# A hybrid encoder layer on one core: the chunk state update as one plain fp32 product, decay factors on ScalarE, the second logits product on 128 rows

## The chip, the cores and the metric

The kernel runs on one core of a Trainium2 chip. The metric is the device time of one execution in microseconds (us); lower is better. Several executions were timed and one was profiled. The core has five engines that run side by side: TensorE (PE: matrix products, with a row of its own for the loading of their stationary operand, PEld), VectorE (DVE), ScalarE (ACT), GpSimd (POOL) and SyncE (SP), which issues the transfers here. SBUF is the working memory, PSUM the memory into which TensorE writes.

## The reference, cut to what matters

One layer for two groups of tokens, 512 of a prompt and 32 of a sample, 1024 wide. A single input projection gives q, k, v for a banded attention and z, x, B, C, dt for a chunked state space scan (32 heads in 4 groups). Then come the output projections, a feed-forward block with a short convolution, and a gated product with a second embedding. The change lies in the scan and in the logits of the attention:

```python
def step(hc, inp):                       # scan over chunks, all heads
    xc, dtc, ac, bc, cc = inp
    acs = jnp.cumsum(ac, axis=1)
    seg = acs[:, :, None] - acs[:, None, :]
    decay = jnp.where(tri, jnp.exp(jnp.where(tri, seg, 0.0)), 0.0)
    cb = jnp.einsum('bign,bjgn->bijg', cc, bc)
    dx = dtc[..., None] * xc
    y = jnp.einsum('bijg,bijgr,bjgrp->bigrp', cb, decay, dx)
    y = y + jnp.einsum('bign,bgrpn->bigrp', cc, hc) * jnp.exp(acs)[..., None]
    last = acs[:, -1]
    wj = jnp.exp(last[:, None] - acs)[..., None] * dx
    h_new = hc * jnp.exp(last)[..., None, None] + jnp.einsum('bjgn,bjgrp->bgrpn', bc, wj)
    return h_new, y

def attend(q, k, v, bias):
    logits = jnp.einsum('bihd,bjhd->bhij', q, k) * (HEAD_DIM_A ** -0.5)
    probs = jax.nn.softmax(logits + bias[None], axis=-1)
    return jnp.einsum('bhij,bjhd->bihd', probs, v)
```

## The kernel before

Features lie on the partitions and the 544 tokens along the free dimension, in two halves of 272. A dense product is a list of steps; one step makes 128 output features, and is cut into pieces of 128 input features. Both operands are split into a high and a low part of a reduced fp32 type (`F32R`), and a piece (`mm3`) is six products of 128 rows and 272 columns: high by high, low by high, high by low, each for two halves. The weights are split as they arrive: ScalarE casts the high part (`wh`, L250), VectorE or GpSimd subtracts it (`wl`, L254), one unit of eight pieces ahead of its use.

All products are issued in one written order on TensorE (class `Ordered` chains them). The order of the other engines is made by a scheduler from the order of the program. The dense steps are the filling: `dense.run(n)` puts n pieces between two parts of other work. So the program has three stretches. In the scan stretch 20 passes (4 groups by 5 chunks, the fifth being the sample) are laid between dense pieces: `ssd_a` of a pass, 7 pieces, `ssd_b` of the pass before, 6 pieces. In the attention stretch parts of the attention (`att_a`: logits and softmax, `att_b`: transposes of the probabilities, `att_c`: their product with v) are laid between dense pieces in the same way. The rest is dense products alone.

`ssd_a` of one pass: C·B and a transpose of B go to one PSUM tile (`cbt`, one of four of a ring that all such work shares, `sps`); L625 masks the first into `cbm`. Four transposes give x by tokens (`xst`), from which L636 makes `dx` and `wj`. `wj` and the transposed B are split in a high and a low part (L627, L628, L640, L641). For each half of the heads the cumulated decay exponents of the chunk, broadcast over the partitions, are loaded (`ab`, L647); four subtractions with a minimum (L651, VectorE, one per head), an exponential (L652, ScalarE) and a product with the mask (L653, VectorE) make `m`; L657 and L658 make the factor for the state from `ab`. `dx`, `wj`, `m`, `ab` and their parts are tiles of one ring of 14 (`half_tile`). `ssd_b`: the y products (`yps`) from `m`, `dx`, `ab` and the state, L684 adds them to x, three products make the new state's share (`st`, L688), and L691 and L693 update the state `h`.

`stack` prepares a head's logits: on the 128 rows of `ks` the high part of k stands twice, and on those of `qs` the high and the low part of q, so that one product of 128 rows gives two of the three. The third, high part of q by low part of k, is a product over the 64 rows of the head itself (L849); the low parts of both heads of a pair share one tile `kl`, each on its own 64 rows.

Of the kernel before, what the change touches and what calls it, by code (L numbers as in the profile page):

```python
# [9 lines left out]
F32 = mybir.dt.float32  # L10
F32R = mybir.dt.float32r
AF = mybir.ActivationFunctionType
# [104 lines left out]
def trunk(ctx: ExitStack, tc: tile.TileContext, a):  # L117
# [433 lines left out]
    def bias_vector():  # L551
        er = const.tile([16, EROW], F32, name="er")
        nc.sync.dma_start(er[:, 383:EROW], a["rb"])
        V.tensor_scalar(er[:, 383:EROW], er[:, 383:EROW], -1.0, None, op0=MUL)
        V.tensor_copy(er[:, 0:383], er[:, 383:384].to_broadcast([16, 383]))
        nc.sync.dma_start(evec, er)
        for h in range(16):
            dense.defer(16 + 16 * h, lambda h=h: bias_rows(h))
# [52 lines left out]
    def ssd_a(g, c):  # L611
# [11 lines left out]
        PE.transpose(sm[:Q, 128:256], b[:, tk], ident)  # L623
        cbm = spt([128, 128], "cbm", 2)
        V.tensor_tensor(cbm[:Q, :Q], sm[:Q, 0:Q], tri[:Q, :Q], op=MUL)  # L625
        bth, btl = (pools["sp"].tile([128, 128], F32R, tag=n, name=n, bufs=2) for n in ("bth", "btl"))
        S.copy(bth[:Q], sm[:Q, 128:256])  # L627
        V.tensor_tensor(btl[:Q], sm[:Q, 128:256], bth[:Q].bitcast(F32), op=SUB)  # L628
        xp = sps("xst")
# [8 lines left out]
        dxf = dx.rearrange("p a b -> p (a b)")  # L638
        wjh, wjl = half_tile("wjh", F32R), half_tile("wjl", F32R)
        S.copy(wjh[:Q], wj[:Q])  # L640
        G.tensor_tensor(wjl[:Q], wj[:Q], wjh[:Q].bitcast(F32), op=SUB)  # L641
        sts = [(l[:Q], r.rearrange("p a b -> p (a b)")[:Q]) for l, r in ((bth, wjh), (bth, wjl), (btl, wjh))]
        ms, cps = [], []
        for hh in range(2):
            ab = half_tile("ab")
            src = asc[c, 8 * g + 4 * hh : 8 * g + 4 * hh + 4, 0:Q]
            nc.sync.dma_start(ab[:, :, :Q], src.unsqueeze(0).to_broadcast([128, 4, Q]))  # L647
            m = half_tile("m")
            for i in range(4):
                hd = 8 * g + 4 * hh + i  # L650
                V.tensor_scalar(m[:Q, i, :Q], ab[:Q, i, :Q], tm[:Q, 1, c, hd : hd + 1], 0.0, op0=SUB, op1=MIN)  # L651
            S.activation(m[:Q, :, :Q], m[:Q, :, :Q], AF.Exp)  # L652
            V.tensor_tensor(m[:Q, :, :Q], m[:Q, :, :Q],  # L653
                            cbm[:Q, :Q].unsqueeze(1).to_broadcast([Q, 4, Q]), op=MUL)
            ms.append(m)
            if inter:
                S.activation(ab[:, :, :Q], ab[:, :, :Q], AF.Exp)  # L657
                G.tensor_tensor(ab[:, :, :Q], ab[:, :, :Q],  # L658
                                cc[:, tk].unsqueeze(1).to_broadcast([128, 4, Q]), op=MUL)
                cps.append(ab)  # L660
        return dxf, sts, ms, cps

    def ssd_b(g, c, dxf, sts, ms, cps):
# [23 lines left out]
        for n, (l, r) in enumerate(sts):  # L687
            PE.matmul(st, lhsT=l, rhs=r, start=n == 0, stop=n == 2)  # L688
        hn = spt([128, 512], "h", 4)
# [113 lines left out]

    stk = {}

    def stack(m, hi):
# [4 lines left out]

        kl = st(512, "kl") if hi == 0 else stk[0][2]
        a0, b0 = 64 * hi, 64 - 64 * hi
# [9 lines left out]
    def att_a(m, i):  # L823
# [15 lines left out]
        for hi in range(2):  # L839
# [5 lines left out]
            else:  # L845
                qs, ks, kl = stk[hi]
                sl = slice(n - 256, n - 128)
                PE.matmul(L[:, :n], lhsT=qs[:, sl], rhs=ks[:, 0:n], start=True, stop=False)
                PE.matmul(L[:, :n], lhsT=qs[own, sl], rhs=kl[own, 0:n], start=False, stop=True)  # L849
            Ls.append(L)  # L850
# [295 lines left out]
    todo = [(m, i) for m in range(NPAIR) for i in range(-1 + m % 2, 4)]  # L1146
    prev = None
    att_load(0)
    stack(0, 0)
# [114 lines left out]
```

## Time and profile before

| | us |
|---|---|
| median of 3 runs | 1412.58 (1412.04 to 1417.83) |
| the profiled execution | 1413.28 |
| its span, from the first to the last instruction | 1411.2 |
| TensorE busy | 1376.0 (98%) |
| VectorE busy | 916.0 (65%) |
| ScalarE busy | 613.4 (43%) |
| GpSimd busy | 352.1 (25%) |

An engine's busy time is a mean over stretches with different limits, so it is read by stretch. Products on TensorE are pipelined: the distance between the starts of two that follow each other says what one costs, not its duration. A product in plain fp32 has two records in the trace.

### The profile page before, as it was taken

To read this page: it belongs to the slowest core of one execution; us is meant where nothing else is said; L and a number is where in the kernel's file an instruction comes from. 1 tells how busy PE (TensorE), PEld (TensorE's weight loads), DVE (VectorE), ACT (ScalarE), POOL (GpSimd) and SP (SyncE) were. 2 spreads that over 40 slices of the span, in tenths; PEclk is the share of its full clock that TensorE was granted. 3 is DMA by queue.
4 is the path that set the end of the run, shared out by engine and by line. 5 is a ranking of instruction groups with operands and counts; after the bars stand their busy time and mean duration, and the time that the engine had idled before them with its cause. 6 is when DMAs were issued, how large, how long until landed. Compare 5 with 4: busy or idle time off the path is not lost.

```text
span 1411.2 us, 26759 instructions
## 1 busy us (share of the span) xinstructions
PE 1376.0 (98%) x11065; PEld 1324.1 (94%) x11065; DVE 916.0 (65%) x1654; ACT 613.4 (43%) x1016; POOL 352.1 (25%) x464
## 2 busy tenths in 40 slices
PE   7998898989999999999999999999999999999998
PEld 7997897989988888889999999999999999999998
DVE  7999999996865555564355334577777537753545
ACT  5444343455566666654244223344444214432342
POOL 5466475464422112210000000023333103310000
PEclk9999999999999999999999999999999999999999
DMA  5723232323443323311222332222222232222221
GB/s 175 241 90 109 87 120 64 116 92 110 132 138 114 103 88 99 103 64 61 90 91 90 122 122 90 91 78 79 85 88 91 90 106 90 91 93 90 90 90 65
DMA packets 41929, 142.16 MB, mean 101 GB/s; under 512 B 9264, under 2 KB 13248, under 8 KB 29520
## 3 DMA queue, kind: packets, MB, share of 16 engines
q1 hardware_dynamic: 41808, 140.46, 29.6%
q8 instruction: 87, 1.43, 0.4%
q14 instruction: 34, 0.28, 0.1%
HBM read 129.27 MB, written 14.31 MB: 102 GB/s over the span
## 4 chain that ended last, share of the span: by engine, by line
PE 81%; DVE 13%; DMA 2%; ACT 2%; issue 1%; POOL 1%; SPq 0%; POOLq 0%; ACTq 0%
PE dps L130 72%; DVE m L651 3%; PE L L130 3%; DVE cv L597 2%; PE O L130 2%; DMA ab<-asc 2%; PE Tp L133 1%; DVE m L653 1%; DVE wl L254 1%; PE yps L130 1%; DVE xs L684 1%; DVE dx L636 1%; DVE wj L636 0%; PE qn L130 0%; DVE h L693 0%
## 5 line engine op out<-in xcount | busy, mean ns | idle before, releaser
L130 PE MATMUL dps<-hi,wh 128*128 128x272 f32 x2960 | 627.9, 294 | 14.9 <-DVE ext L572 14.6
L130 PE MATMUL dps<-lo,wh 128*128 128x272 f32 x2960 | 616.2, 290 | 5.3 <-DVE lo L375 5.3
L130 PE MATMUL dps<-hi,wl 128*128 128x272 f32 x2960 | 615.4, 290 | 2.3 <-DVE wl L254 1.9
L130 PEld LDWEIGHTS dps<-hi,wh 128*128 128x128 f32 x2960 | 467.4, 190 | 26.2 <-issue 18.5
L130 PEld LDWEIGHTS dps<-lo,wh 128*128 128x128 f32 x2960 | 469.0, 190 | 6.1 <-DVE lo L375 6.1
L130 PEld LDWEIGHTS dps<-hi,wl 128*128 128x128 f32 x2960 | 467.8, 189 | 3.1 <-DVE wl L254 2.5
L250 ACT CAST wh<-wr 128x1024 fp32r<-128x1024 f32 x192 | 201.2, 1048 | 379.3 <-PE dps L130 339.4
L254 DVE TENSOR_TENSOR wl<-wr,wh 128x1024 fp32r<-128x1024 f32 x173 | 213.3, 1233 | 48.2 <-ACT wh L250 43.3
L597 DVE SCALAR_TENSOR_TENSOR cv<-ext,hv,cv 128x547 f32<-128x547 f32 x72 | 76.9, 1068 | 2.7 <-ACT cv L594 2.1
L1021 DVE SCALAR_TENSOR_TENSOR ucv<-uext,vec,ucv 128x546 f32<-128x546 f32 x96 | 75.4, 785 | 4.2 <-ACT ucv L1018 2.4
L1014 POOL COPY cfo<-uext 128x2 f32<-128x2 f32 x48 | 10.4, 217 | 262.4 <-DVE uext L571 262.4
L1011 POOL MEMSET uext<- 128x2 f32 x48 | 4.6, 95 | 281.2 <-issue 281.2
L1053 DVE TENSOR_TENSOR x<-x,dps 128x544 f32<-128x544 f32 x24 | 17.3, 722 | 78.2 <-PE dps L130 78.0
L651 DVE TENSOR_SCALAR m<-ab,tm 128x128 f32<-128x128 f32 (+1 forms) x160 | 63.2, 452 | 5.3 <-DMA ab<-asc 5.3
L777 DVE CUSTOM_DVE_ANT_0 P<-L,bias 128x128 f32<-128x128 f32 (+3 forms) x64 | 30.9, 483 | 53.7 <-PE L L130 53.2
L569 DVE TENSOR_TENSOR uext<-dps,rstd 128x272 f32<-128x272 f32 x48 | 21.2, 442 | 63.1 <-PE dps L130 58.5
L254 POOL TENSOR_TENSOR wl<-wr,wh 128x1024 fp32r<-128x1024 f32 x19 | 50.8, 2672 | 44.8 <-ACT wh L250 36.8
L1015 POOL COPY cfo<-uext 128x2 f32<-128x2 f32 x48 | 55.5, 1157 | 0.0
L658 POOL TENSOR_TENSOR ab<-ab,bc 128x512 f32<-128x512 f32 (+1 forms) x32 | 42.5, 1332 | 40.1 <-ACT ab L657 37.8
L652 ACT ACTIVATE m<-m 128x512 f32<-128x512 f32 (+1 forms) x40 | 22.7, 567 | 65.8 <-DVE m L651 65.6
L733 POOL TENSOR_TENSOR ql<-qs,qh 128x544 fp32r<-128x544 f32 x16 | 22.0, 1376 | 103.6 <-ACT qh L732 91.6
L779 ACT ACTIVATE P<-P,sm 128x128 f32<-128x128 f32 (+3 forms) x64 | 36.0, 562 | 23.2 <-DVE sm L777 22.9
(246 smaller groups left out, 1626.4 us busy)
## 6 DMA issues: line engine op xcount, KB each, us to landing
wr<-in_w SPq DMA_DIRECT2D x96, 1024.0 KB, 4.9
ab<-asc SPq DMA_DIRECT2D x32, 256.0 KB, 5.5
bsc<-evec SPq DMA_DIRECT2D x16, 320.0 KB, 7.5
bias<-bsc SPq DMA_DIRECT2D x16, 256.0 KB, 3.5
xin<-in_xT SPq DMA_DIRECT2D x8, 272.0 KB, 5.4
out_o_v<-v SPq DMA_DIRECT2D x8, 272.0 KB, 2.1
out_o_k<-qk SPq DMA_DIRECT2D x8, 272.0 KB, 2.1
x<-in_xT SPq DMA_DIRECT2D x8, 272.0 KB, 4.6
```

What stands on the lines that cost most here:

```text
L130: return self._pin(nc.tensor.matmul(*args, **kw))
L250: cp = S.copy(hi, r)
L254: eng.tensor_tensor(lo, r, hi.bitcast(F32), op=SUB)
L597: V.scalar_tensor_tensor(y[:, :n], ext[:, j : j + n], hv[:, 24 * j + ti : 24 * j + ti + 1], y[:, :n], op0=MUL, op1=ADD)
L651: V.tensor_scalar(m[:Q, i, :Q], ab[:Q, i, :Q], tm[:Q, 1, c, hd : hd + 1], 0.0, op0=SUB, op1=MIN)
L652: S.activation(m[:Q, :, :Q], m[:Q, :, :Q], AF.Exp)
L658: G.tensor_tensor(ab[:, :, :Q], ab[:, :, :Q], cc[:, tk].unsqueeze(1).to_broadcast([128, 4, Q]), op=MUL)
L733: G.tensor_tensor(lo[:, :T], sq[:, :T], hi[:, :T].bitcast(F32), op=SUB)
L777: V.tensor_tensor_reduce(out=P, in0=L, in1=B, scale=1.0, scalar=3e38, op0=ADD, op1=MIN, accum_out=nm[:n])
L779: S.activation(P, P, AF.Exp, scale=-1.0, bias=nm[:n], accum_out=sm[:n])
L1015: G.tensor_copy(cfo[:, i, 2:4], ext[:, UW - 2 : UW])
L1021: V.scalar_tensor_tensor(y[:, :n], ext[:, j : j + n], vec[:, V_FW + 48 * j + i : V_FW + 48 * j + i + 1], y[:, :n], op0=MUL, op1=ADD)
```

## The change

`ssd_a`/`ssd_b`: `wj` and the transposed B are no longer split; the state product is one product of plain fp32 operands (`bt` by `wj`) instead of three of split parts. The mask is applied in place, in the PSUM tile, and L653 (L651 after the change) reads it from there. The four subtractions for `m` become four ACTIVATEs on ScalarE (Relu with scale −1 and a bias operand, L649 after the change), followed by an exponential with scale −1. `stack`: each of the two heads gets a tile of its own for the low part of k (`klz0`, `klz1`), the other 64 rows of which are zeroed once before the attention; the third logits product then runs over all 128 rows. `bias_vector`: the vector of the relative bias is put together in two slots of the general tiles and stored in two pieces.

```diff
     def bias_vector():
-        er = const.tile([16, EROW], F32, name="er")
-        nc.sync.dma_start(er[:, 383:EROW], a["rb"])
-        V.tensor_scalar(er[:, 383:EROW], er[:, 383:EROW], -1.0, None, op0=MUL)
-        V.tensor_copy(er[:, 0:383], er[:, 383:384].to_broadcast([16, 383]))
-        nc.sync.dma_start(evec, er)
+        er, e0 = slot(name="er"), slot(name="e0")
+        nc.sync.dma_start(er[0:16, 0:257], a["rb"])
+        V.tensor_scalar(er[0:16, 0:257], er[0:16, 0:257], -1.0, None, op0=MUL)
+        V.tensor_copy(e0[0:16, 0:383], er[0:16, 0:1].to_broadcast([16, 383]))
+        nc.sync.dma_start(evec[:, 0:383], e0[0:16, 0:383])
+        nc.sync.dma_start(evec[:, 383:EROW], er[0:16, 0:257])
+        done(er, e0)
...
-        cbm = spt([128, 128], "cbm", 2)
-        V.tensor_tensor(cbm[:Q, :Q], sm[:Q, 0:Q], tri[:Q, :Q], op=MUL)
-        bth, btl = (pools["sp"].tile([128, 128], F32R, tag=n, name=n, bufs=2) for n in ("bth", "btl"))
-        S.copy(bth[:Q], sm[:Q, 128:256])
-        V.tensor_tensor(btl[:Q], sm[:Q, 128:256], bth[:Q].bitcast(F32), op=SUB)
+        cbm = sm[:, 0:128]
+        V.tensor_tensor(cbm[:Q, :Q], cbm[:Q, :Q], tri[:Q, :Q], op=MUL)
+        bt = spt([128, 128], "bt", 2)
+        S.copy(bt[:Q], sm[:Q, 128:256])
...
-        wjh, wjl = half_tile("wjh", F32R), half_tile("wjl", F32R)
-        S.copy(wjh[:Q], wj[:Q])
-        G.tensor_tensor(wjl[:Q], wj[:Q], wjh[:Q].bitcast(F32), op=SUB)
-        sts = [(l[:Q], r.rearrange("p a b -> p (a b)")[:Q]) for l, r in ((bth, wjh), (bth, wjl), (btl, wjh))]
+        sts = [(bt[:Q], wj.rearrange("p a b -> p (a b)")[:Q])]
...
-                V.tensor_scalar(m[:Q, i, :Q], ab[:Q, i, :Q], tm[:Q, 1, c, hd : hd + 1], 0.0, op0=SUB, op1=MIN)
-            S.activation(m[:Q, :, :Q], m[:Q, :, :Q], AF.Exp)
+                S.activation(m[:Q, i, :Q], ab[:Q, i, :Q], AF.Relu, scale=-1.0, bias=tm[:Q, 1, c, hd : hd + 1])
+            S.activation(m[:Q, :, :Q], m[:Q, :, :Q], AF.Exp, scale=-1.0)
...
-            PE.matmul(st, lhsT=l, rhs=r, start=n == 0, stop=n == 2)
+            PE.matmul(st, lhsT=l, rhs=r, start=True, stop=True)
...
+    klz = []
+
+    def lo_tiles():
+        for hi in range(2):
+            t = pools["ap"].tile([128, 512], F32R, tag=f"klz{hi}", name=f"klz{hi}", bufs=1)
+            G.memset(t.bitcast(F32), 0.0)
+            klz.append(t)
...
-        kl = st(512, "kl") if hi == 0 else stk[0][2]
+        kl = klz[hi]
...
-                PE.matmul(L[:, :n], lhsT=qs[own, sl], rhs=kl[own, 0:n], start=False, stop=True)
+                PE.matmul(L[:, :n], lhsT=qs[:, sl], rhs=kl[:, 0:n], start=False, stop=True)
...
+    lo_tiles()
     att_load(0)
```

The scheduler orders the engines anew. On VectorE, in the scan, between the evacuation of a dense tile and the convolution behind it, there stood before (`xs<-xs,vec,yps` adds the y products of the pass before; `m<-ab,tm` are the subtractions, `m<-m,cbm` the mask product, `wl` a weight's low part):

```order
L684 SCALAR_TENSOR_TENSOR xs<-xs,vec,yps 128x128 x4
L601 SCALAR_TENSOR_TENSOR xs<-th,cv 128x512
L602 SCALAR_TENSOR_TENSOR xs<-th,cv 128x32
L651 TENSOR_SCALAR m<-ab,tm 128x128 x4
L569 TENSOR_TENSOR ext<-dps,rstd 128x272
L571 TENSOR_TENSOR ext<-dps,rstd 128x240
L572 TENSOR_TENSOR ext<-dps,rstd 128x32
L254 TENSOR_TENSOR wl<-wr,wh 128x1024
L651 TENSOR_SCALAR m<-ab,tm 128x128 x4
L653 TENSOR_TENSOR m<-m,cbm 128x512
```

After the change the same place reads (the numbers of lines are those of the changed kernel, where the mask product is L651):

```order
L651 TENSOR_TENSOR m<-m,cbt 128x512
L682 SCALAR_TENSOR_TENSOR xs<-xs,vec,yps 128x128 x4
L603 SCALAR_TENSOR_TENSOR xs<-th,cv 128x512
L604 SCALAR_TENSOR_TENSOR xs<-th,cv 128x32
L651 TENSOR_TENSOR m<-m,cbt 128x512
L571 TENSOR_TENSOR ext<-dps,rstd 128x272
L573 TENSOR_TENSOR ext<-dps,rstd 128x240
L574 TENSOR_TENSOR ext<-dps,rstd 128x32
L254 TENSOR_TENSOR wl<-wr,wh 128x1024
```

The eight subtractions ahead of and behind the evacuation (`ext`) are gone, and the mask products, which now read the PSUM tile `cbt`, stand ahead of it.

On ScalarE, in the scan, a pass had before (`sq` is a square for a norm, `zt` the gate of z):

```order
L383 ACTIVATE sq<-xs 128x544
L627 CAST bth<-cbt 128x128
L250 CAST wh<-wr 128x1024
L640 CAST wjh<-wj 128x512
L711 ACTIVATE zt<-z 128x544
L383 ACTIVATE sq<-xs 128x544
L652 ACTIVATE m<-m 128x512
L657 ACTIVATE ab<-ab 128x512
L652 ACTIVATE m<-m 128x512
L657 ACTIVATE ab<-ab 128x512
L250 CAST wh<-wr 128x1024
```

After the change the same pass reads:

```order
L383 ACTIVATE sq<-xs 128x544
L629 COPY bt<-cbt 128x128
L250 CAST wh<-wr 128x1024
L649 ACTIVATE m<-ab,tm 128x128 x4
L709 ACTIVATE zt<-z 128x544
L650 ACTIVATE m<-m 128x512
L655 ACTIVATE ab<-ab 128x512
L649 ACTIVATE m<-ab,tm 128x128 x4
L383 ACTIVATE sq<-xs 128x544
L650 ACTIVATE m<-m 128x512
L655 ACTIVATE ab<-ab 128x512
L250 CAST wh<-wr 128x1024
```

Two groups of four subtractions, each of which waits for a load of `ab`, now stand between the casts of two weights; the cast of `wj` is gone.

## Rows read from the trace of the kernel before

**Rows 1.** The page: busy us, share of the span, instructions of each engine.
```profile
PE 1376.0 (98%) x11065; PEld 1324.1 (94%) x11065; DVE 916.0 (65%) x1654; ACT 613.4 (43%) x1016; POOL 352.1 (25%) x464
```

**Rows 2.** Busy time by stretch: length, engines (instructions), granted clock, DMA share, GB/s.
```profile
74.00:387.00 313.00, 289.91 (x2432) 273.51 (x2432) 289.79 (x572) 144.07 (x241) 175.04 (x162) 0.97 0.32 104
387.00:644.00 257.00, 256.63 (x2071) 225.01 (x2072) 145.37 (x365) 158.83 (x384) 48.29 (x48) 1.00 0.30 98
644.00:1411.00 767.00, 762.55 (x6070) 762.01 (x6066) 417.24 (x607) 274.78 (x338) 93.29 (x192) 1.00 0.26 91
...
318.00:355.00 37.00, 36.91 (x314) 35.18 (x314) 25.44 (x56) 19.94 (x36) 16.84 (x11) 0.96 0.38 119
```

**Rows 3.** Waits of PE, 74 to 387 us: total, times, longest.
```profile
PE dps L130 <- DVE ext L572: 14.2, 6, 4.4
```

**Rows 4.** Groups of PE, 74 to 387 us: busy, mean ns | idle before, releaser.
```profile
L130 PE MATMUL dps<-hi,wh 128*128 128x272 f32 x538 | 117.5, 301 | 14.3 <-DVE ext L572 14.2 <-ACT wh L250 0.2
```

**Rows 5.** Timeline of PE and PEld in the scan: start, us, engine, operation.
```profile
198.28 0.44 PE L130 MATMUL yps<-m,dx 128*64 128x128 f32 x4
...
200.18 0.50 PE L130 MATMUL st<-wjh,bth 128*128 128x512 f32 x1
...
200.52 0.39 PE L130 MATMUL st<-wjl,bth 128*128 128x512 f32 x1
...
200.75 0.39 PE L130 MATMUL st<-wjh,btl 128*128 128x512 f32 x1
...
200.98 0.41 PE L130 MATMUL dps<-hi,wh 128*128 128x272 f32 x2
...
205.36 0.31 PEld L130 LDWEIGHTS cbt<-bc 128*128 128x128 f32 x2
...
206.14 0.30 PEld L130 LDWEIGHTS dps<-hi,wh 128*128 128x128 f32 x2
```

**Rows 6.** VectorE's L651 by stretch; tile m (min/median/max ns); groups of DVE.
```profile
74.00:387.00 313.00, 63.17 (x160) 0.97 0.32 104
...
L651 DVE TENSOR_SCALAR m<-ab,tm x160: 219/275/3675, 82.3 to 373.1; 128x128 f32<-128x128 f32 x128, 32x32 f32<-32x32 f32 x32
...
L653 DVE TENSOR_TENSOR m<-m,cbm x40: 271/682/2203, 84.1 to 375.0; 128x512 f32<-128x512 f32 x32, 32x128 f32<-32x128 f32 x8
...
L653 DVE TENSOR_TENSOR m<-m,cbm 128x512 f32<-128x512 f32 x32 | 27.6, 866 | 2.3 <-ACT m L652 2.2
...
L693 DVE TENSOR_TENSOR h<-h,st 128x512 f32<-128x512 f32 x16 | 10.8, 675 | 0.0
```

**Rows 7.** Timeline of DVE in the same pass.
```profile
201.36 3.40 DVE L651 TENSOR_SCALAR m<-ab,tm 128x128 f32<-128x128 f32 x6
...
205.67 1.52 DVE L651 TENSOR_SCALAR m<-ab,tm 128x128 f32<-128x128 f32 x2
207.11 1.11 DVE L684 SCALAR_TENSOR_TENSOR xs<-xs,vec,yps 128x128 f32<-128x128 f32 x4
```

**Rows 8.** Groups of ACT and POOL.
```profile
L627 ACT CAST bth<-cbt 128x128 fp32r<-128x128 f32 x16 | 4.2, 260 | 12.8 <-DVE cbm L625 12.7
...
L779 ACT ACTIVATE P<-P,sm 128x128 f32<-128x128 f32 x16 | 6.4, 402 | 5.5 <-DVE sm L777 5.5
...
L641 POOL TENSOR_TENSOR wjl<-wj,wjh 128x512 fp32r<-128x512 f32 x16 | 24.8, 1553 | 19.7 <-ACT wjh L640 19.7
```

**Rows 9.** Timeline of PE in the attention; the group of second logits products.
```profile
463.17 0.44 PE L130 MATMUL L<-ks,qs 128*128 128x384 f32 x1
463.54 0.44 PE L130 MATMUL L<-kl,qs 64*128 64x384 f32 x1
...
464.65 0.53 PE L130 MATMUL dps<-hi,wh 128*128 128x272 f32 x2
...
L130 PE MATMUL L<-kl,qs 64*128 64x256 f32 (+2 forms) x48 | 21.1, 439 | 0.0
```

**Rows 10.** Tile rps: a plain fp32 product of 128 rows (min/median/max ns, first and last start).
```profile
L130 PE MATMUL rps<-acc,ones x4: 392/392/393, 26.3 to 26.9; 128*128 128x272 f32 x4
```

## The prediction

> **What bounds the kernel now.** The first view is the page: TensorE is busy 1376 of 1411.2 us [rows 1], so only time in which it stands still, or does other work than it must, can be won. The second is the table by stretches [rows 2]. From 644 us on TensorE starts 6070 matmuls in 767 us, 0.126 us each, with nothing between them; the change touches nothing there. In the attention stretch (387 to 644) it is also never idle (256.6 of 257 us). In the scan stretch (74 to 387) it is idle 313 − 289.9 = 23.1 us, its mean granted clock falls to 0.97 (0.03 × 313 = 9.4 us of work), and VectorE is busy 289.8 us, 93%. The third is the waits of TensorE there: the longest is for L572, the last evacuation of a PSUM tile by VectorE [rows 3]. So the scan is bound by VectorE in parts, the attention by TensorE.
>
> How much the scan loses in all I get a second way, from its work. 538 + 539 + 540 dense matmuls (the first of the three groups is in [rows 4]; the other two are alike) at 0.126 are 204 us. Each of the 20 passes has the y products (198.28 to 200.18, 1.90), the state products (200.18 to 200.98, 0.80) and the transposes with C·B (205.36 to 206.14, 0.78) [rows 5]: 20 × 3.48 = 70, less 4 × 0.95 because a first chunk has half of the y products. With some 39 small matmuls of the QK norm and of v (5 us) that is 275, so 38 of 313 us are lost; the idle time and the clock give 32.5. I take 37.
>
> **The change, part by part.**
>
> *Four subtractions per half pass go from VectorE to ScalarE.* On VectorE all 160 take 63.2 us [rows 6]. Their median is 275 ns, but the longest 3675 ns: a large part of their time is not work but waiting while GpSimd runs. In the shown pass six of them hold VectorE for 3.40 us and two more for 1.52 [rows 7]. All 63 us leave VectorE. On ScalarE a 128x128 copy without a bias operand takes 260 ns and a 128x128 ACTIVATE with a bias operand and an accumulator 402 ns [rows 8]: 160 × 0.26 to 0.40 = 42 to 64 us more. I take 0.35, 56 us, between the two since there is a bias and no accumulator. ScalarE is busy 144 of 313 us [rows 2], so it comes to 200 of some 285, 70%; the 20 casts of wj that it loses I leave out. That is hidden behind TensorE; without that cover it would be up to 56 us.
>
> A rule of the Trainium skill speaks against this part: "ScalarE: Activation LUTs", section Rules for kernel authors, says to use VectorE and not ScalarE for relu, min and add. By the rule alone the scan would pay those 56 us. What the rows show is the opposite state: VectorE full and ScalarE at 46%.
>
> *The split parts go.* VectorE loses 20 subtractions of btl, 128 columns each; at the median of a subtraction for m, which is as long, that is 20 × 0.275 = 5.5 us. GpSimd loses 20 of wjl, 1.553 us each [rows 8], 32 of its 175 busy us, and with them so many stretches in which VectorE is held up.
>
> *The mask product reads PSUM.* L653 takes 866 ns in the mean over its 32 full sizes, and 682 at the median [rows 6]. With one operand in PSUM the nearest row is L693, 675 ns, which hardly varies. So between nothing and 32 × 0.19 = 6 us less; I take 6, since L693 has the same shape and the same place of its operands. VectorE then has 290 − 63 − 6 − 6 = 215 us of work left in the scan, and less by what wjl held up: 75% of 285. In the stretch 318 to 355 it was at 69% and TensorE ran through (36.91 of 37 us) [rows 2].
>
> The product of m has the cbt tile as operand, so this PSUM tile of four is held until the second product of its pass, where it was free after btl. This is the one new wait; its price is under the rivals. The operand tiles of a pass fall from 8 to 6 of a ring of 14, so the loads of ab are issued earlier; I give no gain for this apart from the one below.
>
> So of the 37 us I expect three quarters back, **−28**. A quarter stays: the hand-over from scan to attention, waits for ab, and the new PSUM order.
>
> *The state product becomes one plain fp32 product.* Now three products stand 0.23 us apart (200.52, 200.75, 200.98) [rows 5], 0.69 us. The trace has a plain fp32 product of 128 rows: the sum over squares, two records per product; four records of 272 columns start from 26.3 to 26.9 [rows 10], 0.20 apart. For 512 columns that is 2 × 0.20 × 512/272 = 0.75 us. The starts are rounded to 0.1, so the distance is 0.17 to 0.23 and the product 0.64 to 0.87 us: 20 times −1 to +4 us. I take **+2**. The Trainium skill, "FP8 and Floating Point Precision", section TensorE Precision Notes, says that true fp32 is four passes through the array; four passes at 0.23 would be 0.92 us, and the term +4.6 in place of +2.
>
> *The second logits product on 128 rows.* For 384 columns the four products start 0.37 us apart: 463.17, 463.54, and 464.65 for the dense matmul behind the fourth [rows 9], 1.48 us. The state products, which all have 128 rows, take 0.23 us for 512 columns, so 0.17 for 384; each logits product thus costs 0.20 us more than its columns, at each change between 128 and 64 rows. The first state product, behind y products of 64 columns, has 0.34 [rows 5], 0.11 more. After the change I expect 0.28 + 3 × 0.17 = 0.80 us, 0.68 less. There are 48 such second products [rows 9], 24 groups of two: **−16.3 us**. If the gap has nothing to do with the rows it is 0; if the first is also without a gap, 24 × 0.8 = 19. This stretch has TensorE on the path throughout, VectorE at 57% and ScalarE at 62% [rows 2], so I let all of it count. Beside the row, the Trainium skill, "TensorEngine Tiling (Array Packing)", section Key Properties, says that a change of the tiling mode drains TensorE; the 0.20 us agree with it.
>
> *Cost nothing:* the zeroing of the two klz tiles (two memsets on GpSimd, which is idle then; up to 3 us if the first kl were waited for, at 1.5 us for an operation of 128x512 [rows 8]), and the bias vector in two stores instead of one (issued some 300 us before the first bias tile is read, under dense work; SP has nothing behind it that is late).
>
> **Sum.** Profiled execution 1413.3 us; −28 + 2 − 16.3 = −42.3: 1371.0. The median of the runs is 0.7 lower, so **1370 us**.
>
> **The rivals.**
>
> 1. *The scan keeps its stalls.* What took the time of VectorE was a chain of waits, and after the change it is ScalarE's queue: four subtractions wait for ab, and behind them stands the cast wh for the dense work. For it: it is one engine in order. Against: ScalarE at 70%, and each weight is cast a whole unit ahead. Then only 8 of 37 come back: 1413.3 − 8 + 2 − 16 − 1 = 1390.
> 2. *The scan loses nothing any more*, as between 318 and 355, and the logits gain 19: 1413 − 37 + 1 − 19 − 1 = 1357, or 1352 if the 275 us were too many.
> 3. *The logits keep their gaps*, because these come from something else than the number of rows (the change does not do what it says): 1413 − 28 + 2 − 1 = 1386.
> 4. *Slower:* the held PSUM tile. The transposes of the next pass now wait for the last L684 of the pass before (or for its second mask product). In the shown pass that L684 ends at 208.22 [rows 7], 2.1 us after the transposes were done at 206.14 [rows 5]. If this lag stayed, 20 × 2.1 = 42 us: 1413 + 42 + 2 − 16 = 1441. It decides when VectorE is more than about 6 us behind the y products (200.18 to 206.14). In that pass it was 8.0 behind, but 3.40 + 1.52 of it were the subtractions that go, which leaves 3.1. So it is unlikely.
>
> **How the numbers follow.** Forecast (1360 to 1381) 0.55; rival 1 0.20; rival 2 0.13; rival 3 0.07; rival 4 or less of it 0.03; others 0.02. The range holds the first three rivals' centres and the bounds of the state product and the logits: 1352 to 1393. What this kernel's measurement can tell from no change is 0.5%, 7 us. Only rival 4 and a part of the others end at 1406 or more: faster 0.94, same 0.03, slower 0.03.
>
> **What would show it.** Right: four logits products of 384 columns in about 0.80 us; the state product in about 0.75 us; between 74 and the end of the scan VectorE at some 75%, ScalarE at some 70%, TensorE's idle time and clock loss under 12 us; the scan some 26 us shorter, the attention some 16. Wrong: waits of TensorE at the transposes for L682 or the mask product (rival 4), ACT wh as the releaser of TensorE (rival 1), or logits products still 0.37 apart (rival 3).

## The result, and the profile after

The changed kernel takes **1369.21 us** (median of 4 runs, 1367.78 to 1369.60), the kernel before 1412.94 (4 runs, 1412.04 to 1417.83): a ratio of 0.968, 95% interval 0.966 to 0.971. The prediction was 1370.

The page of the changed kernel, busy us, share of the span (1367.5 us) and instructions of each engine, answers to [rows 1]:

```profile
PE 1350.5 (99%) x11045; PEld 1311.3 (96%) x11045; DVE 848.5 (62%) x1474; ACT 643.3 (47%) x1156; POOL 318.2 (23%) x446
```

The table by stretches answers to [rows 2] (length, then PE, PEld, DVE, ACT, POOL, clock, DMA share, GB/s); the scan now ends near 361, the attention near 602 us:

```profile
74.00:361.00 287.00, 284.37 (x2427) 265.19 (x2426) 220.39 (x393) 176.14 (x382) 141.38 (x145) 0.99 0.35 114
...
361.00:602.00 241.00, 239.42 (x2076) 223.42 (x2075) 149.60 (x365) 157.90 (x385) 47.25 (x48) 1.00 0.32 103
...
602.00:1367.00 765.00, 760.75 (x6055) 760.39 (x6053) 415.59 (x606) 273.51 (x335) 95.22 (x192) 1.00 0.27 91
```

In the scan TensorE is idle 2.6 us where it was idle 23.1, at a mean granted clock of 0.99 where it was 0.97. VectorE went from 93% to 77%, ScalarE from 46% to 61%. All of TensorE's waits in the scan are in one line (total, times, longest), where [rows 3] had 14.2 us for the evacuation of `ext` alone:

```profile
PE st L130 <- DVE xs L682: 2.6, 2, 1.3
```

Where the time came from is best measured between marks that both traces have. From the first state product to the last: 92.8 to 378.9 before, 93.5 to 351.65 after, −27.9 us. From there to the last product of probabilities by v (`O`): 378.9 to 644.3 before, 351.65 to 600.8 after, −16.2. From there to the end of the span −0.2, ahead of the first mark +0.7. That is −43.6 of the −43.7 between the spans. Of the 27.9 us of the scan, 20.5 are idle time of TensorE that is gone; its busy time there also fell, from 263.0 to 255.7 us, though the new state product is dearer, at a mean granted clock of 0.99 where it was 0.96 (the rows stand under e9).

The timeline of TensorE after, around one state product and around the four logits products of 384 columns (start, us), answers to [rows 5] and [rows 9]:

```profile
201.56 0.39 PE L130 MATMUL yps<-ab,h 128*64 128x128 f32 x4
201.87 1.13 PE L130 MATMUL st<-wj,bt 128*128 128x512 f32 x2
202.44 0.82 PE L130 MATMUL dps<-hi,wh 128*128 128x272 f32 x2
203.09 0.41 PE L130 MATMUL dps<-lo,wh 128*128 128x272 f32 x2
...
457.21 0.44 PE L130 MATMUL L<-ks,qs 128*128 128x384 f32 x1
457.49 0.34 PE L130 MATMUL L<-klz,qs 128*128 128x384 f32 x1
457.66 0.34 PE L130 MATMUL L<-ks,qs 128*128 128x384 f32 x1
457.83 0.34 PE L130 MATMUL L<-klz,qs 128*128 128x384 f32 x1
458.01 0.41 PE L130 MATMUL dps<-hi,wh 128*128 128x272 f32 x2
```

The logits group takes 458.01 − 457.21 = 0.80 us, with the products 0.17 apart; before it was 1.48 [rows 9]. The state product needs more care: behind it stands not only its own time, for the second dense group starts 0.65 us after the first where 0.25 is usual. So it is measured up to that second group: 203.09 − 201.87 = 1.22 us. Before, the same distance ran from 200.18 [rows 5] to

```profile
201.22 0.41 PE L130 MATMUL dps<-lo,wh 128*128 128x272 f32 x2
```

in the timeline of the kernel before, 1.04 us. The plain product costs 0.18 us more than the three passes in this pass; in most others the two distances are 1.21 and 1.05 us, so 0.16 to 0.18, and 20 × 0.17 = 3.4 us in all.

The tile m after (min/median/max ns), beside [rows 6]:

```profile
L649 ACT ACTIVATE m<-ab,tm x160: 304/387/407, 80.9 to 340.4; 128x128 f32<-128x128 f32 x128, 32x32 f32<-32x32 f32 x32
...
L651 DVE TENSOR_TENSOR m<-m,cbt x40: 265/678/691, 82.7 to 343.5; 128x512 f32<-128x512 f32 x32, 32x128 f32<-32x128 f32 x8
```

On ScalarE a subtraction lasts 387 ns and never more than 407; on VectorE the median was 275, but single ones lasted 3675. The mask product, with one operand in PSUM, now never lasts more than 691 ns; it went up to 2203 before.

### The profile page after: what moved, and what is told of

It reads as the page before. It is cut to its first block, busy times and chain, and to the rows that moved or that the text cites. A ratio compares the mean times of both kernels' runs of the same rounds, so it can differ in the third digit from the quotient of the medians.

```text
span 1367.5 us, 26629 instructions
## 1 busy us (share of the span) xinstructions
PE 1350.5 (99%) x11045; PEld 1311.3 (96%) x11045; DVE 848.5 (62%) x1474; ACT 643.3 (47%) x1156; POOL 318.2 (23%) x446
## 4 chain that ended last, share of the span: by engine, by line
PE 96%; DVE 1%; ACT 1%; DMA 0%; issue 0%; SPq 0%; DVEq 0%; ACTq 0%
PE dps L130 84%; PE yps L130 3%; PE O L130 2%; PE L L130 2%; PE st L130 2%; PE Tp L133 1%; PE xst L133 1%; DVE qs L824 1%; PE qn L130 0%; PE gps L130 0%; DMA xin<-in_xT 0%; PE cbt L130 0%; PE vt L133 0%; ACT wh L250 0%; ACT P L777 0%
## 5 line engine op out<-in xcount | busy, mean ns | idle before, releaser
L599 DVE SCALAR_TENSOR_TENSOR cv<-ext,hv,cv 128x547 f32<-128x547 f32 x72 | 68.7, 954 | 5.8 <-ACT cv L596 5.0
L254 POOL TENSOR_TENSOR wl<-wr,wh 128x1024 fp32r<-128x1024 f32 x19 | 47.5, 2500 | 58.4 <-ACT wh L250 58.4
L649 ACT ACTIVATE m<-ab,tm 128x128 f32<-128x128 f32 (+1 forms) x160 | 48.3, 374 | 4.9 <-DMA ab<-asc 4.9
L777 ACT ACTIVATE P<-P,sm 128x128 f32<-128x128 f32 (+3 forms) x64 | 35.9, 561 | 23.7 <-DVE sm L775 23.5
L368 ACT CAST hi<-me 128x544 fp32r<-128x544 f32 x24 | 15.5, 647 | 61.9 <-DVE me L1044 61.9
```

The costliest lines, as they stand in the source:

```text
L254: eng.tensor_tensor(lo, r, hi.bitcast(F32), op=SUB)
L599: V.scalar_tensor_tensor(y[:, :n], ext[:, j : j + n], hv[:, 24 * j + ti : 24 * j + ti + 1], y[:, :n], op0=MUL, op1=ADD)
L649: S.activation(m[:Q, i, :Q], ab[:Q, i, :Q], AF.Relu, scale=-1.0, bias=tm[:Q, 1, c, hd : hd + 1])
L777: S.activation(P, P, AF.Exp, scale=-1.0, bias=nm[:n], accum_out=sm[:n])
```

## The experiments

The open question is not the size but the cause: the change does several things at once to the scan. **Theory 1**: VectorE's queue was too full, and the subtractions, its largest part, had to leave it. **Theory 2**: GpSimd's `wjl` held VectorE up, and its end gave the gain. Further rivals: ScalarE's queue, the ring of 14 tiles, the held PSUM tile.

### e1: the logits alone

```diff
-        kl = st(512, "kl") if hi == 0 else stk[0][2]
+        kl = klz[hi]
...
-                PE.matmul(L[:, :n], lhsT=qs[own, sl], rhs=kl[own, 0:n], start=False, stop=True)
+                PE.matmul(L[:, :n], lhsT=qs[:, sl], rhs=kl[:, 0:n], start=False, stop=True)
```

> The kernel before with only the logits part of the change (own tiles for the low part of k, third product on 128 rows, bias vector in two stores). If the gap belongs to the change between 128 and 64 rows: 0.68 us for each of 24 groups, 1413 - 16.5 = 1396.5 us, and four products of 384 columns in 0.80 us. If the gain of the attention stretch in the full change came from somewhere else (weights and engines relieved earlier): no more than 3 us, 1410.

Measured: 1398.03 us against 1414.12 of the kernel before beside it (ratio 0.988, 0.986 to 0.991), −16.1 us. The timeline of TensorE in e1 has a group of 384 columns in 489.76 − 488.96 = 0.80 us:

```profile
488.96 0.44 PE L130 MATMUL L<-ks,qs 128*128 128x384 f32 x1
...
489.76 0.41 PE L130 MATMUL dps<-hi,wh 128*128 128x272 f32 x2
```

From the last state product to the last `O` e1 takes 249.1 us (383.5 to 632.6) where the kernel before took 265.4: the logits part stands by itself and gives what was forecast.

### e2, e3: each part of the scan alone

e2, before with the subtractions on ScalarE:

```diff
-                V.tensor_scalar(m[:Q, i, :Q], ab[:Q, i, :Q], tm[:Q, 1, c, hd : hd + 1], 0.0, op0=SUB, op1=MIN)
-            S.activation(m[:Q, :, :Q], m[:Q, :, :Q], AF.Exp)
+                S.activation(m[:Q, i, :Q], ab[:Q, i, :Q], AF.Relu, scale=-1.0, bias=tm[:Q, 1, c, hd : hd + 1])
+            S.activation(m[:Q, :, :Q], m[:Q, :, :Q], AF.Exp, scale=-1.0)
```

> The kernel before with only the subtractions for m moved to ScalarE. Theory 1 (the scan lost its time because VectorE was full, and the subtractions are what filled it): VectorE falls from 290 to some 227 busy us in the scan, most of the stalls go, 1413 - 25 = 1388 us. Theory 2 (it was GpSimd's wjl that held VectorE up, and its end is what the full change gains from): wjl is still there, 1413 - 8 = 1405 us. Theory 3 (ScalarE's queue takes the stalls over as long as it casts wjh too): 1408 or more.

e3, before with the plain state product (the lines that make `bth`, `btl`, `wjh` and `wjl` go too and are left out here):

```diff
-        sts = [(l[:Q], r.rearrange("p a b -> p (a b)")[:Q]) for l, r in ((bth, wjh), (bth, wjl), (btl, wjh))]
+        sts = [(bt[:Q], wj.rearrange("p a b -> p (a b)")[:Q])]
```

> The kernel before with only the state product in plain fp32 (no bth, btl, wjh, wjl). The product itself costs 20 times 0.17 = 3.4 us more by the trace after the change. Theory 1: VectorE loses 5.5 us of btl and perhaps 15 us of hold-ups in the subtractions, the scan wins some 10: 1413 - 10 + 3 = 1406 us. Theory 2: the hold-ups were the cause, the scan wins 25: 1413 - 25 + 3 = 1391 us; the longest subtraction for m would fall from 3675 ns to under 1000.

Measured: e2 1390.29 us (0.982, 0.979 to 0.985), e3 1388.90 (0.982, 0.979 to 0.984); before 1414.12. Each part alone wins 24 to 25 us, and the whole change wins no more than some 28 in the scan. The parts do not add: either one ends most of the stalls. e2 came out as theory 1 says, e3 as theory 2 says, though its longest subtraction did not fall under 1000 ns as theory 2 wanted (tile m of e3):

```profile
L647 DVE TENSOR_SCALAR m<-ab,tm x160: 219/275/2466, 80.9 to 348.4; 128x128 f32<-128x128 f32 x128, 32x32 f32<-32x32 f32 x32
```

The gain of e3 lies not in the subtractions alone. Its convolution `cv` on VectorE, which [rows 6] did not list, fell too: by groups of VectorE in the scan, first before, then e3:

```profile
L597 DVE SCALAR_TENSOR_TENSOR cv<-ext,hv,cv 128x547 f32<-128x547 f32 x51 | 58.4, 1145 | 2.0 <-ACT cv L594 1.6
```

```profile
L597 DVE SCALAR_TENSOR_TENSOR cv<-ext,hv,cv 128x547 f32<-128x547 f32 x51 | 46.0, 901 | 1.6 <-ACT cv L594 1.3
```

The same 51 instructions take 12.4 us less once the split parts are gone, so it was not the subtractions only that were held up. A single hold-up can be seen in the pass of [rows 7], in the timeline of the kernel before:

```profile
198.00 2.85 POOL L254 TENSOR_TENSOR wl<-wr,wh 128x1024 fp32r<-128x1024 f32 x1
198.66 2.78 DVE L713 TENSOR_TENSOR xs<-xs,z 128x544 f32<-128x544 f32 x1
200.81 1.77 POOL L641 TENSOR_TENSOR wjl<-wj,wjh 128x512 fp32r<-128x512 f32 x1
```

The product of VectorE, 0.72 us at the median of its 16, starts while GpSimd works on a weight (`wl`) and ends 0.59 us after GpSimd's instruction does (the spans of GpSimd in a profile are rough). So `wjl` was not the only instruction of GpSimd that held VectorE up, and not every operation gained when it went: the mask product, 27.6 us before [rows 6], takes 29.8 in e3:

```profile
L649 DVE TENSOR_TENSOR m<-m,cbm 128x512 f32<-128x512 f32 x32 | 29.8, 931 | 3.1 <-ACT m L648 2.8
```

### e4: the change with the subtractions back on VectorE

```diff
-                S.activation(m[:Q, i, :Q], ab[:Q, i, :Q], AF.Relu, scale=-1.0, bias=tm[:Q, 1, c, hd : hd + 1])
-            S.activation(m[:Q, :, :Q], m[:Q, :, :Q], AF.Exp, scale=-1.0)
+                V.tensor_scalar(m[:Q, i, :Q], ab[:Q, i, :Q], tm[:Q, 1, c, hd : hd + 1], 0.0, op0=SUB, op1=MIN)
+            S.activation(m[:Q, :, :Q], m[:Q, :, :Q], AF.Exp)
```

> The changed kernel with the subtractions for m back on VectorE. Theory 1: VectorE is back at over 260 busy us of the scan and its evacuations are late again, 1369 + 18 = 1387 us. Theory 2: without wjl the subtractions take about 0.25 us each, 40 us in all, and hurt nobody, 1369 + 3 = 1372 us.

Measured: 1367.82 us (0.967, 0.964 to 0.969), the same as the change. With the rest of the change in place, moving 160 operations to ScalarE is worth nothing: on VectorE they now take 50.8 us instead of 63.2. Theory 1 as stated here (over 260 busy us, late evacuations) falls. What TensorE waited for in the scan of e4:

```profile
PE xst L133 <- DVE m L651: 3.7, 3, 1.8
PE dps L130 <- DVE ext L574: 0.5, 1, 0.5
```

The first line is rival 4 of the prediction: the transposes wait for a mask product, which holds the PSUM tile. It costs 3.7 us.

### e5, e6: GpSimd's subtraction left out, and the ring

e5, before without the instruction for `wjl`:

```diff
-        wjh, wjl = half_tile("wjh", F32R), half_tile("wjl", F32R)
+        wjh = half_tile("wjh", F32R)
         S.copy(wjh[:Q], wj[:Q])
-        G.tensor_tensor(wjl[:Q], wj[:Q], wjh[:Q].bitcast(F32), op=SUB)
...
-... ((bth, wjh), (bth, wjl), (btl, wjh))]
+... ((bth, wjh), (bth, wjh), (btl, wjh))]
```

> The kernel before, where the low part of wj is left out and the second state product repeats the first (TensorE's work is unchanged, the subtractions for m stay on VectorE, wjh and btl stay; the output lacks that part). Theory 2 (VectorE is held up by GpSimd's wjl, and any relief of some 25 us of its time ends the stalls): VectorE's time for m and for the convolution cv falls as in the state part alone (63 to 51 and 58 to 46 us), 1413 - 20 = 1393 us. Theory 4 (the state part alone helped because it takes 6 instead of 8 tiles of the ring of 14, so the loads of ab start earlier): 7 of 14 is half of that step, 1413 - 10 = 1403 us or more. Theory 5 (it helped by the work of ScalarE and VectorE for wjh and btl): 1410 us.

e6, before with a larger ring:

```diff
-        return pools["sp"].tile([128, 4, 128], dt, tag="c", name=name, bufs=14)
+        return pools["sp"].tile([128, 4, 128], dt, tag="c", name=name, bufs=18)
```

> The kernel before with 18 instead of 14 tiles in the ring that dx, wj, wjh, wjl, ab and m share. Theory 4 (the ring holds the loads of ab back): the scan wins as much as by the state part, 1413 - 20 = 1393 us. Theory 2: VectorE waited for loads of ab only 3.7 us in the scan before, 1413 - 3 = 1410 us.

Measured, against 1416.42 of the kernel before: e5 1399.68 (0.988, 0.985 to 0.992), e6 1416.38 (1.000, 0.999 to 1.002). The ring by itself does nothing; theory 4 falls in that form. `wjl` alone gives back 17 us, less than the 25 of the whole state part and between the numbers of theories 2 and 4. The subtractions fell to 55.0 us and the mean of `cv` to 1006 ns, not to e3's 51.0 and 901 as theory 2 had it, and the wait for `ext` is still there in the scan of e5:

```profile
PE dps L130 <- DVE ext L572: 9.3, 5, 4.9
```

The rest of the state part's gain belongs to what else it drops: `btl` on VectorE (5.6 us), `wjh` on ScalarE, one more tile of the ring. Which of these, no run here separates.

### e9: VectorE filled again without GpSimd

e9, the change with the subtractions on VectorE as in e4, and each of them issued twice:

```diff
-                S.activation(m[:Q, i, :Q], ab[:Q, i, :Q], AF.Relu, scale=-1.0, bias=tm[:Q, 1, c, hd : hd + 1])
-            S.activation(m[:Q, :, :Q], m[:Q, :, :Q], AF.Exp, scale=-1.0)
+                V.tensor_scalar(m[:Q, i, :Q], ab[:Q, i, :Q], tm[:Q, 1, c, hd : hd + 1], 0.0, op0=SUB, op1=MIN)
+                V.tensor_scalar(m[:Q, i, :Q], ab[:Q, i, :Q], tm[:Q, 1, c, hd : hd + 1], 0.0, op0=SUB, op1=MIN)
+            S.activation(m[:Q, :, :Q], m[:Q, :, :Q], AF.Exp)
```

> The changed kernel with the subtractions for m on VectorE as in e4, each issued twice with the same result (no wjl, no btl: GpSimd's load is that of the change). They add some 45 us of VectorE's time, so that it has as much as before the change. Theory 1 (the stalls come when VectorE's queue is too full, whatever fills it): TensorE waits for ext again, by 20 us or more: 1368 + 25 = 1393 us or above. Theory 2 in its narrow form (only GpSimd's wjl makes the stalls): no new waits, 1368 to 1372 us.

Measured: 1399.69 us (0.989, 0.987 to 0.991 against before; the change beside it, e12, 1368.53). The stalls are back in full, +31 us, with GpSimd as light as in the change (124.3 us between the marks against 128.2). The waits of TensorE up to 354 us, the longest three:

```profile
PE dps L130 <- DVE ext L574: 9.4, 2, 7.1
PE xst L133 <- DVE xs L683: 6.4, 2, 5.0
PE dps L130 <- DVE z L708: 4.4, 1, 4.4
```

So theory 2 in its narrow form falls as well. What brings the stalls is how much lies in VectorE's queue, whoever put it there: own work or hold-ups. The rows by stretch from the first state product to the last show it, in one column, the busy time of DVE: before, e3, the change, e9.

```profile
92.80:378.90 286.10, 263.01 (x2205) 247.49 (x2201) 265.05 (x523) 130.75 (x218) 160.85 (x147) 0.96 0.30 100
```

```profile
93.70:356.30 262.60, 257.82 (x2185) 238.35 (x2183) 238.85 (x498) 118.40 (x198) 137.74 (x126) 0.99 0.33 108
```

```profile
93.50:351.80 258.30, 255.67 (x2187) 237.68 (x2184) 195.95 (x349) 159.10 (x346) 128.24 (x122) 0.99 0.33 110
```

```profile
91.90:381.40 289.50, 264.37 (x2185) 244.65 (x2184) 272.59 (x650) 121.62 (x200) 124.33 (x126) 0.96 0.30 98
```

The same view of every run, in order of VectorE's busy time (with the plain product the stretch holds 19 × 0.17 = 3.2 us more of TensorE's own work):

| kernel | VectorE busy us | length of the stretch | state product |
|---|---|---|---|
| e9 | 272.6 | 289.5 | plain |
| e6 | 267.0 | 287.9 | three passes |
| e1 | 265.7 | 289.9 | three passes |
| before | 265.1 | 286.1 | three passes |
| e5 | 252.9 | 272.5 | three passes |
| e3 | 238.9 | 262.6 | plain |
| e4 | 233.4 | 258.9 | plain |
| e11 | 226.1 | 261.9 | three passes |
| e2 | 223.2 | 264.2 | three passes |
| e8 | 208.3 | 255.6 | plain |
| e7 | 206.7 | 260.2 | three passes |
| the change | 196.0 | 258.3 | plain |

Each length is that of one profiled execution. The scan of e1 is that of the kernel before, and yet its stretch is 3.8 us longer, at a mean granted clock of 0.94 where it was 0.96; the change and its repetition e12 differ by 0.1. So a few us between two single rows mean little where there are stalls. From 265 to 239 us nearly each us that leaves VectorE shortens the scan by one (26 of VectorE, 23.5 of the scan, though the plain product adds 3.2). Below that there is little left to buy: 43 us more, down to 196, are worth 4. The three runs with three passes below that (e2, e11, e7) lie 1 to 9 us above the plain ones, though TensorE has less work in them, so there VectorE's sum alone does not set the length.

### e7, e8, e11, e12: the price of the other parts, and a better version

e7, the change with the three passes again (and `bth`, `btl`, `wjh`, `wjl` as before, whose lines are left out here):

```diff
-        sts = [(bt[:Q], wj.rearrange("p a b -> p (a b)")[:Q])]
+        sts = [(l[:Q], r.rearrange("p a b -> p (a b)")[:Q]) for l, r in ((bth, wjh), (bth, wjl), (btl, wjh))]
```

> The changed kernel with the state product in three passes of split parts again (wjl on GpSimd, btl on VectorE, wjh on ScalarE, 8 tiles of 14), the subtractions for m still on ScalarE. By the products alone 20 times 0.17 less: 1369.2 - 3.4 = 1366 us. Theory 2 with room (VectorE has some 50 us to spare since the subtractions left it): wjl holds it up by 20 us, btl adds 6, and nobody waits: 1366 us. If GpSimd's hold-ups hurt wherever they fall: 1369 + 5 = 1374 us or more.

e8, the change with the masked C·B in SBUF:

```diff
-        cbm = sm[:, 0:128]
-        V.tensor_tensor(cbm[:Q, :Q], cbm[:Q, :Q], tri[:Q, :Q], op=MUL)
+        cbm = spt([128, 128], "cbm", 2)
+        V.tensor_tensor(cbm[:Q, :Q], sm[:Q, 0:Q], tri[:Q, :Q], op=MUL)
```

> The changed kernel with the masked C.B copied to SBUF again, so that the mask product has no operand in PSUM and the PSUM tile is free early. If an operand in PSUM keeps the product clear of GpSimd's hold-ups: its 32 full sizes go from 0.68 us, none above 0.70, back to a mean of over 0.8 with some above 2 us, VectorE has 8 us more, and the time rises by 1 to 5, 1372 us. If holding the PSUM tile costs something in the change: 1366 us. If neither: 1369 us.

e11, e8 with the three passes as in e7, but `wjl` on VectorE (only its difference from e7 and e8 is shown):

```diff
-        G.tensor_tensor(wjl[:Q], wj[:Q], wjh[:Q].bitcast(F32), op=SUB)
+        V.tensor_tensor(wjl[:Q], wj[:Q], wjh[:Q].bitcast(F32), op=SUB)
```

> A version to beat the change: mask in SBUF as in e8, subtractions for m on ScalarE, the state product again in three passes of split parts, but wjl on VectorE and not on GpSimd. VectorE gets 20 x 0.68 + 20 x 0.28 = 19 us more, 248 of 280 us, and is not held up by wjl. If that is still room enough: e8 less 20 x 0.17, 1366.8 - 3.4 = 1363.4 us. If VectorE or ScalarE (wjh is back, 13 us) is late again: 1370 us or more.

e12, the change itself beside e9 to e11:

> The changed kernel itself, on the chip of the runs beside it, so that small differences can be told: 1369 us.

Measured: e7 1370.15 us (0.968, 0.965 to 0.971), e8 1366.75 (0.965, 0.962 to 0.968), e11 1373.50 (0.970, 0.968 to 0.972), e12 1368.53 (0.967, 0.965 to 0.970).

e7 answers neither number: the 3.4 us of the cheaper product do not show, and the time is that of the change. Its row between the marks, to be read beside that of the change:

```profile
94.40:354.60 260.20, 256.08 (x2204) 244.28 (x2202) 206.66 (x372) 171.82 (x370) 153.77 (x145) 0.97 0.33 111
```

TensorE is idle 4.1 us where it was idle 2.6 (it waits 2.8 us for ScalarE's `qs` and 1.1 for VectorE's `xs`), and for less work it is busy as long, at a granted clock of 0.97 where it was 0.99. The profiled execution is the slowest of the four of e7; what the other three, at a higher clock, lost, no trace shows. e11 is a miss: 5 us slower than the change beside it, with three new waits for `ext` (3.4 us) and again a clock of 0.97, though VectorE was busy less than in e4. So its busy time is not all; `wjl`, which must wait for ScalarE's cast, stands in its queue, perhaps ahead of work that TensorE needs. That is argued from the waits, no run shows it apart.

e8 tells two things. First, its mask product, both operands in SBUF, takes longer again (groups of VectorE in the scan, in e8 and in the change):

```profile
L651 DVE TENSOR_TENSOR m<-m,cbm 128x512 f32<-128x512 f32 x32 | 34.7, 1084 | 15.8 <-ACT m L650 15.8
```

```profile
L651 DVE TENSOR_TENSOR m<-m,cbt 128x512 f32<-128x512 f32 x32 | 21.8, 680 | 12.0 <-ACT m L650 11.8
```

Second, with 13 us more of VectorE's time for it the scan is not longer but 2.7 us shorter, for TensorE has no wait left (length, PE busy):

```profile
93.00:348.60 255.60, 255.60 (x2185) 237.65 (x2183) 208.29 (x348) 158.80 (x347) 134.27 (x122) 0.99 0.34 111
```

The two waits of the change, `st` for `xs`, 2.6 us, are gone once the PSUM tile is free early. By the trace e8 is the best version; by the times it can't be told from the change, the intervals of the ratios overlap (0.962 to 0.968, and 0.965 to 0.970 for e12).

### e10: a state product by itself, and logits on 64 rows throughout

```diff
-        for n, (l, r) in enumerate(sts):
+        for n, (l, r) in enumerate(sts + sts):
...
-                PE.matmul(L[:, :n], lhsT=qs[:, sl], rhs=ks[:, 0:n], start=True, stop=False)
-                PE.matmul(L[:, :n], lhsT=qs[:, sl], rhs=kl[:, 0:n], start=False, stop=True)
+                PE.matmul(L[:, :n], lhsT=qs[own, sl], rhs=ks[own, 0:n], start=True, stop=False)
+                PE.matmul(L[:, :n], lhsT=qs[own, sl], rhs=kl[own, 0:n], start=False, stop=True)
```

> The changed kernel with two edits in different stretches: the state product is issued twice with the same result, and all logits products of a group run on the 64 rows of their head (the product of the low part of q is left out, so the output lacks it). Scan: a plain fp32 product of 512 columns costs 0.86 us by the distance of starts after the change, so the scan gets 20 x 0.86 = 17 us longer; by the 0.75 of the prediction 15. Attention: if the gap belongs to the change between 128 and 64 rows, four products of 384 columns stand 0.17 us apart inside the group and only its two ends have a gap, some 1.1 us from the first to the dense product behind, 24 x 0.3 = 7 us more than the change: 1393 us in all. If products on 64 rows are slow in themselves, they stand 0.37 us apart, 1.5 us or more in all: 24 x 0.7 = 17 us, 1403 us in all.

Measured: 1385.20 us (0.979, 0.976 to 0.981), 16.7 more than e12. The timeline of TensorE in e10, a doubled state product and a group of 384 columns:

```profile
205.79 1.99 PE L130 MATMUL st<-wj,bt 128*128 128x512 f32 x4
207.21 0.81 PE L130 MATMUL dps<-hi,wh 128*128 128x272 f32 x2
207.86 0.41 PE L130 MATMUL dps<-lo,wh 128*128 128x272 f32 x2
...
472.36 0.44 PE L130 MATMUL L<-ks,qs 64*128 64x384 f32 x2
472.64 0.33 PE L130 MATMUL L<-klz,qs 64*128 64x384 f32 x2
472.90 0.53 PE L130 MATMUL dps<-hi,wh 128*128 128x272 f32 x2
473.27 0.41 PE L130 MATMUL dps<-lo,wh 128*128 128x272 f32 x2
```

The two state products take 207.86 − 205.79 = 2.07 us where one took 1.22, so a plain fp32 product of 512 columns costs 0.85 us, not 0.75. From the first state product to the last e10 takes 274.5 us (92.10 to 366.61), 16.4 more than the change; 19 × 0.86 is 16.3. And products on 64 rows are not slow in themselves: the gap belongs to the change between 128 and 64 rows, as the prediction had it. They even came closer than expected: four products of 384 columns in 0.54 us. The tile L of e10 in that group (first and last start) shows why: the products of the two heads start together.

```profile
L130 PE MATMUL L<-ks,qs x2: 437/437/437, 472.4 to 472.4; 64*128 64x384 f32 x2
...
L130 PE MATMUL L<-klz,qs x2: 327/328/328, 472.6 to 472.6; 64*128 64x384 f32 x2
```

So the stretch from the last state product to the last `O` is 247.9 us long (366.61 to 614.5), 1.3 less than in the change where 7 more had been expected, and that is why the time lies below the 1393 of the expectation.

## Why the prediction was right, step by step

**The logits, −16.3.** Measured −16.1 alone (e1) and −16.2 in the full change. Four products in 0.80 us, as worked out. The reading of the gap as one for each change of rows is shown by e10, where it vanishes with 64 rows throughout. Rival 3 falls.

**The state product, +2.** Mis-sized, though inside its bounds of −1 to +4: 0.17 us for each product, 20 × 0.17 = 3.4. (Its own 0.75 us would have given 20 × 0.06 = 1.2; the +2 was a choice.) The distance of 0.20 came from the first and last start in [rows 10], which are rounded to 0.1 us. The timeline of the same four products in the kernel before has it finer:

```profile
26.25 1.08 PE L130 MATMUL rps<-acc,ones 128*128 128x272 f32 x4
```

The last of the four lasts 0.39 us [rows 10], so it starts at 26.94: three distances in 0.69 us, 0.23 each. For 512 columns that is 2 × 0.23 × 512/272 = 0.87 us, and the term would have been 20 × (0.87 − 0.69) = +3.6. The Trainium skill, "FP8 and Floating Point Precision", section TensorE Precision Notes, has four passes for true fp32. The trace is near it: 0.85 is four times 0.21 us, where one pass of the split parts was 0.23 [rows 5].

**The stalls of the scan, −28.** The scan between the marks is 27.9 us shorter, with 3.2 us of dearer products in it: 31 us came back instead of 28, 20.5 of them as idle time, the rest as busy time that shrank with the higher clock. The quarter that was to stay was a choice, and it was too much; by the prediction's own count TensorE's idle time and clock loss are now 2.6 + 0.01 × 287 = 5.5 us. The +2 was 1.4 us too low and the −28 some 3 us too small a gain; that the two errors point in opposite directions is why the sum came out within 1 us of the measured median, and that much of it is luck.

The size was right, and so was the cause named, a full queue of VectorE: e9 fills it again and the stalls return. The account of what empties it was too simple. Of the some 75 us of relief that the prediction priced, 63 were the subtractions. The runs show two remedies for one full queue, of which either does most of it: without the subtractions −24 us (e2), without the split parts −25 us (e3), and with the other parts in place the move to ScalarE is worth nothing (e4). What the prediction held for a side effect, the end of `wjl`, is the larger part of a remedy of the same size (17 of 25 us, e5), since GpSimd held up not only `m` but the convolution too.

**The terms of VectorE and ScalarE.** Subtractions on ScalarE 0.387 us at the median, 48.3 us in all (taken: 0.35, 56 us). VectorE at 77% of the scan (75% forecast), ScalarE at 61% (70%; the casts of `wj` that the prediction left out are 12 us of that, 118.4 us of ScalarE between the marks in e3 against 130.8 before): no TensorE wait there ends at ScalarE, and rival 1 falls. The rule of "ScalarE: Activation LUTs" in the Trainium skill, section Rules for kernel authors, against relu on ScalarE: e4 beside the change shows that here it makes no difference, either way, at 1367.8 and 1368.5 us. The mask product gained 5.8 us of VectorE's time (27.6 to 21.8; 6 forecast) and e8 shows that these bought nothing while the subtractions are on ScalarE. With them on VectorE it may be otherwise: e4 is 5 us below what e3 and e1 give if their gains add (1414.1 − 25.2 − 16.1 = 1372.8). No run has the mask in PSUM by itself.

**Rival 4, the held PSUM tile.** It is there, at 2.6 us in the change, where the state product waits for a PSUM tile, and 3.7 in e4, where the transposes do, not 42: VectorE is no longer late enough. In e9, where it is late again, the transposes wait 6.4 us. e8, which frees the tile early, has none of it.

**Rival 2.** Of its two parts the scan comes near: e8 has no wait left, and its scan is 2.7 us shorter than the change's. The logits gained 16.2, not 19, so its 1357 us stay far off.

## What to carry to other kernels

A queue that is too full costs about what it is over, and below that little: here 26 us off VectorE were worth 23.5, and the next 43 worth 4. So find how much must leave, then do the cheapest of the remedies, since they don't add. Here dropping the split parts gave 25 us and the logits 16, together nearly all of the 43.7; no run has just these two, but e4, which has only the mask in PSUM besides, takes no longer than the change. Look for operations whose longest time is many times their median, as 3675 ns beside 275 here: an engine's busy share can hold waiting for another engine, and a timeline of both shows for which. And before a term is taken from the distance of records, read their starts from the timeline and not from rounded figures, and where a record's end is hidden, look at when the second instruction behind it starts.

## What the runs showed of the hardware that was not expected

- The VectorE product with one operand in PSUM was in no case held up in these traces, though GpSimd was busy 141 us of the scan: at most 691 ns for `m<-m,cbt` in the change, 2493 ns for the same product with both operands in SBUF in e8:

```profile
L651 DVE TENSOR_TENSOR m<-m,cbm x40: 273/688/2493, 82.1 to 341.8; 128x512 f32<-128x512 f32 x32, 32x128 f32<-32x128 f32 x8
```

  The Trainium skill, "SBUF — State Buffer", section SBUF: two separate sides, says that an operation of VectorE with two inputs in SBUF can be blocked by a GpSimd operation that reads SBUF. By that rule one input in PSUM is enough to be free of it, and the trace agrees.
- TensorE ran products on the upper and on the lower 64 rows side by side: four products of 384 columns from 472.36 to 472.90 in e10, started in pairs, where four in a row on 128 rows take 0.80 us. "TensorEngine Tiling (Array Packing)" in the Trainium skill, section Key Properties, says that different tiles execute in parallel; the trace agrees.
- The plain fp32 product of 512 columns costs 0.85 us (e10), the three passes of split parts some 0.69 (0.23 each [rows 5]).
